# First projection weights loaded between the modulation's parts, modulation as columns, k tiles multiplied as they come

## The chip, the cores and the metric

The kernel runs on one core of a Trainium2 chip. Its engines work side by side, each through its own queue in order: TensorE (PE) multiplies, VectorE (DVE) and ScalarE (ACT) do the elementwise work, GpSimd (POOL) and SyncE (SP) mostly issue transfers. The metric is the device time of one execution in microseconds (us), as the median of several runs.

## The reference

One transformer layer for 512 tokens of width 1024 in f32: modulation from a condition vector, one projection to all branches, sparse attention and a state-space branch beside each other, their mix, and 32 experts of which each token takes four. The change touches its first lines only:

```python
cond = jax.nn.silu(c)
mod = cond @ w_ada[l] + b_ada[l]
sh_m, sc_m, g_m, sh_f, sc_f, g_f = jnp.split(mod[:, None, :], 6, axis=-1)
h = _rms(x, norm_mix[l]) * (1.0 + sc_m) + sh_m
proj = h @ w_in[l]
...
```

## The kernel before

A framework schedules the program: the source states the work, and the scheduler decides in which order each engine gets its instructions; the queues then run in that order and wait on semaphores. Tiles come from pools with few buffers (`raw`, `whi` and `wlo` have two each), and a tile's next use waits until the one before has been read.

*The modulation.* `sc_m` and `sh_m` are needed as columns (channel on the partition) in `mod1`: columns 8 to 15 hold the scale, 0 to 7 the shift. The weights come in four parts `early[j]`, j = 0 to 3, of 256 channels each; a part has a scale tile set `early[j][0]` and a shift tile set `early[j][1]` of 1 MB each. Their buffers are called bE (part 0, and again part 3), bV (part 1) and bD (part 2). `modulation(j)` computes the scale as a row, eight matmuls with `cond` as weights and 256 moving columns (L328), copies the row to SBUF on ACT (L330) and turns it into columns with matmuls against a one (L335). The shift is accumulated on DVE over the eight k tiles (`mac`, L255 and L257) and summed over partitions by L336. Three small DVE operations (L338 to L340) finish the part. An f32 matmul shows as two records in the trace.

*The input.* `xs0` (buffer bC) holds the 512 tokens as four tiles. ACT squares and sums them (L310), DVE computes the inverse root (L311, then `rsqrt`, L237 to L242) and scales bC (L314).

*The operand.* `modulate(j)` transposes channels 256 j to 256 j + 255 (L346; two k tiles, eight transposes), ACT applies scale and shift twice (L347 to the rounded high part in `hT[0]`, buffer bA; L349), and DVE subtracts for the low part (L350, buffer B).

*The projection.* A product of f32 quality is made of three matmuls of 512 columns (L356 to L358: high x high, low x high, high x low). `project` does so for a list of outputs and a list of k tiles. `first` is three outputs: 88 rows from `w_small` into bank sy, and two of 128 rows from `w_in[0]` into the banks mm: 8 x 3 x 3 = 72 matmuls. The last two outputs come from `w_in[1]` (banks ss): 48 matmuls. Weights are loaded by `load` (L176, on SP's queue, in the order of the source) and parted by `split` (L182 on ACT, L183 on DVE); `w_small` by `hilo` (L247, L248).

*Behind the stage.* The 88-row output is copied and transposed (L426, L433, L434), the index keys are normalized and transposed (L451), and the next weights are split by `advance`. From there on PE has projections, attention and experts up to the end.

Of the kernel before, what the change touches and what calls it, by code (L numbers as in the profile page):

```python
# [16 lines left out]
AF = mybir.ActivationFunctionType  # L17
OP = mybir.AluOpType
# [4 lines left out]
P = 128  # L23
# [3 lines left out]
KD = D // P  # L27
# [106 lines left out]
def program(tc, A, dbg=None, upto=99):  # L134
    nc = tc.nc
    V, S, T, G = nc.vector, nc.scalar, nc.tensor, nc.gpsimd
# [3 lines left out]
    with ctx:  # L140
# [14 lines left out]
        c_c, b_a1, nmix, gain, ssmn, convc, dskip = (cols[:, a:b] for a, b in (  # L155
            (0, 8), (8, 24), (24, 32), (32, 38), (38, 46), (46, 106), (106, 114)))
        identb = con.tile([P, P], BF, name="identb")
        V.tensor_copy(identb, ident)
        ones = con.tile([P, P], F32, name="ones")
# [14 lines left out]
        def load(src, n=2048, pool=None):  # L174
            raw = (pool or stm).tile([P, 2048], F32, name="raw", tag="raw", bufs=RAW)
            nc.sync.dma_start(raw[:, 0:n], src)  # L176
            return raw

        def split(raw, n=2048, pin=False):
            hi = stm.tile([P, 2048], F32R, name="whi", tag="whi", bufs=HI)  # L180
            lo = stm.tile([P, 2048], F32R, name="wlo", tag="wlo", bufs=LO)
            S.activation(hi[:, 0:n], raw[:, 0:n], AF.Copy)  # L182
            i = V.tensor_tensor(lo[:, 0:n], raw[:, 0:n], hi[:, 0:n].bitcast(F32), op=OP.subtract)  # L183
            if pin:
                tc.keep_in_program_order(i)
            return hi, lo
# [18 lines left out]
        with ExitStack() as c1:  # L205
# [4 lines left out]
            c0 = ExitStack()  # L210
            WE = c0.enter_context(tc.tile_pool(name="WE", bufs=1, side="right"))

            def big(tag, shape, dt=F32):
                return (WE if tag in ("E", "V", "V2", "SC", "S8") else W).tile(shape, dt, name=f"b{tag}", tag=tag, bufs=1)
# [7 lines left out]
            def r2(shape=(P, 512), dt=F32, name="r2"):  # L222
                return W.tile(list(shape), dt, name=name, tag="r2", bufs=R2)
# [4 lines left out]
            def sm(shape, dt=F32, name="sm", bufs=2):  # L228
                return W.tile(list(shape), dt, name=name, tag=name, bufs=bufs)

            def pt(tag, shape=(P, 512), dt=F32):
                return ps.tile(list(shape), dt, name=tag, tag=tag, bufs=PS[tag])
# [20 lines left out]
            def mac(acc, tiles):  # L253

                V.tensor_scalar(acc, part(tiles, 0), cond[:, 0:1], None, op0=OP.mult)  # L255
                for k in range(1, KD):
                    V.scalar_tensor_tensor(acc, part(tiles, k), cond[:, k:k + 1], acc, op0=OP.mult, op1=OP.add)  # L257
# [11 lines left out]
            def two(tag):  # L269
                t2 = big(tag, [P, 2, 2048])  # L270
                return [t2[:, 0]], [t2[:, 1]]

            early = [two("E"), ([big("V", [P, 2048])], [big("V2", [P, 2048])])]
# [5 lines left out]
            def ada_load(tiles, j):  # L279
                for i in range(2):  # L280
                    n = 2048 // len(tiles[i])
                    for h, tile_ in enumerate(tiles[i]):
                        nc.sync.dma_start(tile_, A["w_ada"][j + 4 * (1 - i)][:, h * n:(h + 1) * n])
                return tiles

            def part(tiles, k):
                n = KD // len(tiles)
                return tiles[k // n][:, (k % n) * 256:(k % n + 1) * 256]

            ada_load(early[0], 0)  # L290
            for t in range(NT):
                nc.sync.dma_start(xs0[:, t, :], xv[:, t, :])
            ada_load(early[1], 1)
            ada_load(early[2], 2)
            raws = [load(A["w_small"][0], KD * 88), load(A["w_in"][0])]
            heads = con.tile([P, 32], F32, name="heads")
            nc.scalar.dma_start(heads, _bcast(A["heads"], 32))
            rel = con.tile([32, 8], F32, name="rel")
# [3 lines left out]
            cond = con.tile([P, KD], F32, name="cond")  # L302
# [14 lines left out]
            wqi = [split(raws[1])]  # L317

            ada = pt("ac")
            mod1 = con.tile([P, 16], F32, name="mod1")  # L320
            psm = pt("sy")
            pqi = [pt("mm"), pt("mm"), pt("ss"), pt("ss")]

            def modulation(j):
                row = sm([1, 256], name="brow", bufs=1)
                p = ada[0:1, 256:512]
                for k in range(KD):
                    T.matmul(p, cond[:, k:k + 1], part(early[j][0], k),  # L328
                             start=(k == 0), stop=(k == KD - 1))
                S.activation(row, p, AF.Copy)  # L330
                acc = r2((P, 256))
                mac(acc, early[j][1])
                for b in range(2):
                    n = 2 * j + b
                    T.matmul(ada[:, 8 + n:9 + n], row[:, b * P:(b + 1) * P], ones[0:1, 0:1], start=True, stop=True)  # L335
                    T.matmul(ada[:, n:n + 1], acc[:, b * P:(b + 1) * P], ones[:, 0:1], start=True, stop=True)  # L336
                n = 2 * j
                V.tensor_tensor(mod1[:, 8 + n:10 + n], ada[:, 8 + n:10 + n], b_a1[:, 8 + n:10 + n], op=OP.add)  # L338
                V.tensor_tensor(mod1[:, n:n + 2], ada[:, n:n + 2], b_a1[:, n:n + 2], op=OP.add)
                V.scalar_tensor_tensor(mod1[:, 8 + n:10 + n], mod1[:, 8 + n:10 + n], 1.0, nmix[:, n:n + 2], op0=OP.add, op1=OP.mult)  # L340

            def modulate(j):
                for k in (2 * j, 2 * j + 1):
                    p = pt("at")
                    for t in range(NT):
                        T.transpose(p[:, t * P:(t + 1) * P], xs0[:, t, k * P:(k + 1) * P], ident)  # L346
                    S.activation(hT[0][:, k, :], p, AF.Identity, bias=mod1[:, k:k + 1], scale=mod1[:, 8 + k:9 + k])  # L347
                    f = r2()
                    S.activation(f, p, AF.Identity, bias=mod1[:, k:k + 1], scale=mod1[:, 8 + k:9 + k])  # L349
                    V.tensor_tensor(hT[1][:, k, :], f, hT[0][:, k, :].bitcast(F32), op=OP.subtract)  # L350

            def project(outs, ks):
                for k in ks:
                    for p, (wh, wl), step, c0, m in outs:
                        c = k * step + c0
                        T.matmul(p, wh[:, c:c + m], hT[0][:, k, :], start=(k == 0), stop=False)  # L356
                        T.matmul(p, wh[:, c:c + m], hT[1][:, k, :], start=False, stop=False)
                        T.matmul(p, wl[:, c:c + m], hT[0][:, k, :], start=False, stop=(k == KD - 1))  # L358

            first = [(psm[0:88, :], wsm, 88, 0, 88)] + [(pqi[c], wqi[0], 256, c * P, P) for c in range(2)]  # L360
            for j in range(4):
                modulation(j)
                if j == 0:
                    early.append(ada_load(two("E"), 3))
                    raws.append(load(A["w_in"][1]))
                if j > 0:
                    modulate(j - 1)
                if j > 1:
                    project(first, (2 * j - 4, 2 * j - 3))
            modulate(3)  # L370
            project(first, range(4, KD))
            wqi.append(split(raws[2]))
            for c in range(2, 4):
                project([(pqi[c], wqi[1], 256, (c % 2) * P, P)], range(KD))
            say("hT_hi", hT[0].bitcast(F32), [P, KD, L])
            for i in range(2):
                say(f"hT_lo{i}", hT[1].tiles[i].bitcast(F32), [P, 4, L])
# [53 lines left out]
            p = pt("at", (P, NT, P))  # L431
# [12 lines left out]
            for t in range(NT):  # L444
                for b in range(2):
                    V.tensor_scalar(kin[:, t, b * 64:(b + 1) * 64], s88[:, t, 0:64], mv[:, t, 0:1], rski[:, t:t + 1],
                                    op0=OP.subtract, op1=OP.mult)
            kiT = big("K", [P, L])
            p = pt("at")
# [563 lines left out]
            for half in range(2):  # L1013
# [3 lines left out]
                for j2 in range(2):  # L1017
# [4 lines left out]
                    for b in range(2):  # L1022
                        p = pt("mm")
# [13 lines left out]
            for j in range(4):  # L1037
# [9 lines left out]
                for b in range(2):  # L1047
# [3 lines left out]
                    p = pt("mm")  # L1051
# [126 lines left out]
            p = pt("mm")  # L1178
# [4 lines left out]
            p = pt("mm")  # L1183
# [392 lines left out]
        with ExitStack() as c3:  # L1576
# [10 lines left out]
            with tc.For_i(0, nb):  # L1587
# [72 lines left out]
                for n in range(2):  # L1660
                    p = op.tile([P, 512], F32, name="dn", tag="dn", bufs=2)
# [23 lines left out]
```

## Time and profile before

| what | value |
|---|---|
| median of three runs | 1811.93 us (1810.32 to 1813.92) |
| the profiled execution | 1815.36 us |
| its span | 1813.6 us, 22580 instructions |
| mean granted TensorE clock | 0.975 of full speed |

The profile is of one execution, which took 3.4 us more than the median. PE is busy for 97% of the span, DVE for 85% and ACT for 59%; the stage that the change touches is the first 70 us. In the views of the trace each line has a start and a length in us; an engine's idle time stands in brackets with what ended it, and a weight load (PEld) has its own lines beside the matmuls (PE).

### The profile page before, as it was taken

What the parts mean: (1) busy time and instruction counts of PE and PEld (TensorE: products, weight loads), DVE (VectorE), ACT (ScalarE), POOL (GpSimd) and SP (SyncE); (2) the same over time, 40 slices, a digit from 0 to 9 for tenths busy, and PEclk for the clock granted to TensorE, in tenths of its full rate; (3) what the DMA queues carried; (4) which work ended last, traced back from release to release, by engine and by line L of the source; (5) the groups of instructions that cost most, each with busy time, mean ns of one, the idle gap of its engine ahead of it and who ended that gap; (6) DMA issues with size and microseconds to landing.
All of it is one profiled execution on the core that took longest, in us unless ns stands there. A gap on an engine that the chain in (4) does not pass through costs nothing.

```text
span 1813.6 us, 22580 instructions
## 1 busy us (share of the span) xinstructions
PE 1752.4 (97%) x8534; PEld 1389.9 (77%) x8536; DVE 1542.5 (85%) x1886; ACT 1074.8 (59%) x1059; POOL 196.4 (11%) x115
## 2 busy tenths in 40 slices
PE   6999999999999798999999999999999999999997
PEld 3866877776678677888888888888888888888885
DVE  6477678875676789999999999999999999999996
ACT  3444333444323356777777777777777777777774
POOL 0000000000000101111211211111111111211112
PEclk9989999999799899999999999999999999999999
DMA  8232344432485489999999999999999999999993
GB/s 330 73 140 71 118 149 142 163 137 82 141 291 198 152 282 370 395 388 363 381 385 384 381 370 388 375 384 371 374 383 390 353 397 381 365 384 390 381 358 68
DMA packets 86600, 527.24 MB, mean 291 GB/s; under 512 B 10929, under 2 KB 11089, under 8 KB 32217
## 3 DMA queue, kind: packets, MB, share of 16 engines
q1 hardware_dynamic: 70552, 469.70, 66.3%
q0 software_dynamic: 15696, 55.97, 11.3%
q8 instruction: 68, 1.11, 0.2%
q14 instruction: 44, 0.35, 0.1%
q10 hardware_dynamic: 240, 0.10, 0.0%
HBM read 497.91 MB, written 30.45 MB: 291 GB/s over the span
## 4 chain that ended last, share of the span: by engine, by line
PE 88%; DVE 6%; DMA 3%; ACT 2%; issue 1%; SPq 0%; POOLq 0%; DVEq 0%; ACTq 0%
PE gu L1502 12%; PE gu L1500 12%; PE gu L1501 12%; PE dn L1500 7%; PE dn L1502 7%; PE dn L1501 6%; PE mm L393 4%; PE mm L394 4%; PE mm L395 4%; PE tr L1271 3%; PE gu L1511 2%; PE ac L850 1%; PE at L822 1%; DMA xg<-h2d,gi 1%; PE mm L385 1%
## 5 line engine op out<-in xcount | busy, mean ns | idle before, releaser
L1320 DVE TENSOR_TENSOR mlo<-raw,mhi 128x2048 fp32r<-128x2048 f32 (+1 forms) x160 | 352.2, 2205 | 24.3 <-ACT mhi L1319 22.4
L1320 DVE TENSOR_TENSOR wlo<-raw,whi 128x2048 fp32r<-128x2048 f32 x154 | 351.8, 2286 | 24.2 <-ACT whi L1319 22.5
L1319 ACT ACTIVATE whi<-raw 128x2048 fp32r<-128x2048 f32 x154 | 296.2, 1924 | 112.8 <-PE gu L1502 63.2
L1319 ACT ACTIVATE mhi<-raw 128x2048 fp32r<-128x2048 f32 (+1 forms) x160 | 296.6, 1859 | 104.8 <-PE gu L1502 58.4
L1501 PE MATMUL gu<-mlo,xh 128*128 128x512 f32 x496 | 193.3, 390 | 1.5 <-DVE mlo L1320 1.5
L1502 PE MATMUL gu<-whi,xl 128*128 128x512 f32 x496 | 193.8, 391 | 0.0
L1500 PE MATMUL gu<-mhi,xh 128*128 128x512 f32 x496 | 193.8, 391 | 0.0
L1502 PE MATMUL gu<-mhi,xl 128*128 128x512 f32 x496 | 193.8, 391 | 0.0
L1500 PE MATMUL gu<-whi,xh 128*128 128x512 f32 x496 | 193.8, 391 | 0.0
L1501 PE MATMUL gu<-wlo,xh 128*128 128x512 f32 x496 | 193.3, 390 | 0.0
L1290 POOL DMA_INDIRECT out_dram<-y,si x30 | 100.8, 3358 | 444.6 <-DVE y L1560 444.6
L394 PE MATMUL mm<-B,whi 128*128 128x512 f32 x352 | 141.9, 403 | 0.0
L393 PE MATMUL mm<-bA,whi 128*128 128x512 f32 x320 | 132.1, 413 | 2.0 <-DVE brow L662 1.0
L395 PE MATMUL mm<-bA,wlo 128*128 128x512 f32 x320 | 128.7, 403 | 0.8 <-DVE wlo L183 0.8
L182 ACT ACTIVATE whi<-raw 128x2048 fp32r<-128x2048 f32 x34 | 64.9, 1913 | 88.7 <-PE mm L394 74.8
L1377 POOL DMA_INDIRECT xg<-h2d,gi x32 | 59.7, 1866 | 503.0 <-PE tr L1271 479.5
L1501 PEld LDWEIGHTS gu<-mlo,xh 128*128 128x128 f32 x496 | 93.2, 188 | 22.2 <-DVE mlo L1320 1.9
L1501 PEld LDWEIGHTS gu<-wlo,xh 128*128 128x128 f32 x496 | 93.1, 188 | 20.4
L1502 PEld LDWEIGHTS gu<-mhi,xl 128*128 128x128 f32 x496 | 93.1, 188 | 20.2
L1502 PEld LDWEIGHTS gu<-whi,xl 128*128 128x128 f32 x496 | 93.1, 188 | 20.2
L1500 PEld LDWEIGHTS gu<-mhi,xh 128*128 128x128 f32 x496 | 93.1, 188 | 19.5
L1500 PEld LDWEIGHTS gu<-whi,xh 128*128 128x128 f32 x496 | 93.1, 188 | 19.3
(473 smaller groups left out, 3705.9 us busy)
## 6 DMA issues: line engine op xcount, KB each, us to landing
raw<-in_w_gu_dram SPq DMA_DIRECT2D x204, 1024.0 KB
raw<-in_w_dn_dram SPq DMA_DIRECT2D x104, 1024.0 KB
B<-in_w_gu_dram SPq DMA_DIRECT2D x52, 1024.0 KB
B<-in_w_dn_dram SPq DMA_DIRECT2D x24, 1024.0 KB
raw<-in_w_in_dram SPq DMA_DIRECT2D x23, 1024.0 KB
rawp<-in_w_ada_dram POOLq DMA_DIRECT2D x30, 512.0 KB, 4.1
bE<-in_w_ada_dram SPq DMA_DIRECT2D x4, 1024.0 KB
bC<-in_x_dram SPq DMA_DIRECT2D x8, 512.0 KB
```

The costliest lines, as they stand in the source:

```text
L182: S.activation(hi[:, 0:n], raw[:, 0:n], AF.Copy)
L393: T.matmul(p, wh, xT[0][:, k, :], start=(k == 0), stop=False)
L394: T.matmul(p, wh, xT[1][:, k, :], start=False, stop=False)
L395: T.matmul(p, wl, xT[0][:, k, :], start=False, stop=(k == nk - 1))
L1271: T.transpose(p[:, k, :], src[:, (4 * b + k) * P:(4 * b + k + 1) * P], ident)
L1290: return G.indirect_dma_start(out=out, out_offset=bass.IndirectOffsetOnAxis(ap=si, axis=0), in_=y, in_offset=None, compute_op=OP.add)
L1319: S.activation(hi[:, cs], raw[:, cs], AF.Copy)
L1320: i = V.tensor_tensor(lo[:, cs], raw[:, cs], hi[:, cs].bitcast(F32), op=OP.subtract)
L1377: G.indirect_dma_start(out=xg, out_offset=None, in_=h2d, in_offset=bass.IndirectOffsetOnAxis(ap=info[e][0], axis=0))
L1500: T.matmul(p, x[0][:, kk, :], hi[:, ws], start=(start and kk == 0), stop=False)
L1501: T.matmul(p, x[0][:, kk, :], lo[:, ws], start=False, stop=False)
L1502: T.matmul(p, x[1][:, kk, :], hi[:, ws], start=False, stop=(kk == KD - 1))
```

## The change

The scale of every part, and the shift of parts 0 and 1, are now computed as columns: for each half b and each k tile a 128x128 piece of the modulation's weights is the stationary operand and `cond[:, k]` the only moving column, 16 matmuls per tile set. The shifts of parts 2 and 3 stay on DVE. `w_small` and `w_in[0]` are loaded ahead of part 1's tile sets and `w_in[1]` ahead of part 2's. After each part, its two k tiles are transposed and multiplied into the first three outputs at once; at part 2 `w_in[1]` is split and its outputs start, with k tiles 0 to 3, then 4 and 5, and 6 and 7 at the end.

```diff
@@ -290,9 +290,10 @@
             ada_load(early[0], 0)
             for t in range(NT):
                 nc.sync.dma_start(xs0[:, t, :], xv[:, t, :])
+            raws = [load(A["w_small"][0], KD * 88), load(A["w_in"][0])]
             ada_load(early[1], 1)
+            raws.append(load(A["w_in"][1]))
             ada_load(early[2], 2)
-            raws = [load(A["w_small"][0], KD * 88), load(A["w_in"][0])]
             heads = con.tile([P, 32], F32, name="heads")
             nc.scalar.dma_start(heads, _bcast(A["heads"], 32))
             rel = con.tile([32, 8], F32, name="rel")
@@ -322,22 +323,25 @@
             pqi = [pt("mm"), pt("mm"), pt("ss"), pt("ss")]
 
             def modulation(j):
-                row = sm([1, 256], name="brow", bufs=1)
-                p = ada[0:1, 256:512]
-                for k in range(KD):
-                    T.matmul(p, cond[:, k:k + 1], part(early[j][0], k),
-                             start=(k == 0), stop=(k == KD - 1))
-                S.activation(row, p, AF.Copy)
-                acc = r2((P, 256))
-                mac(acc, early[j][1])
-                for b in range(2):
-                    n = 2 * j + b
-                    T.matmul(ada[:, 8 + n:9 + n], row[:, b * P:(b + 1) * P], ones[0:1, 0:1], start=True, stop=True)
-                    T.matmul(ada[:, n:n + 1], acc[:, b * P:(b + 1) * P], ones[:, 0:1], start=True, stop=True)
                 n = 2 * j
+
+                def columns(c0, tiles):
+                    for b in range(2):
+                        for k in range(KD):
+                            T.matmul(ada[:, c0 + b:c0 + b + 1], part(tiles, k)[:, b * P:(b + 1) * P], cond[:, k:k + 1],
+                                     start=(k == 0), stop=(k == KD - 1))
+
+                columns(8 + n, early[j][0])
                 V.tensor_tensor(mod1[:, 8 + n:10 + n], ada[:, 8 + n:10 + n], b_a1[:, 8 + n:10 + n], op=OP.add)
+                V.scalar_tensor_tensor(mod1[:, 8 + n:10 + n], mod1[:, 8 + n:10 + n], 1.0, nmix[:, n:n + 2], op0=OP.add, op1=OP.mult)
+                if j < 2:
+                    columns(n, early[j][1])
+                else:
+                    acc = r2((P, 256))
+                    mac(acc, early[j][1])
+                    for b in range(2):
+                        T.matmul(ada[:, n + b:n + b + 1], acc[:, b * P:(b + 1) * P], ones[:, 0:1], start=True, stop=True)
                 V.tensor_tensor(mod1[:, n:n + 2], ada[:, n:n + 2], b_a1[:, n:n + 2], op=OP.add)
-                V.scalar_tensor_tensor(mod1[:, 8 + n:10 + n], mod1[:, 8 + n:10 + n], 1.0, nmix[:, n:n + 2], op0=OP.add, op1=OP.mult)
 
             def modulate(j):
                 for k in (2 * j, 2 * j + 1):
@@ -358,20 +362,21 @@
                         T.matmul(p, wl[:, c:c + m], hT[0][:, k, :], start=False, stop=(k == KD - 1))
 
             first = [(psm[0:88, :], wsm, 88, 0, 88)] + [(pqi[c], wqi[0], 256, c * P, P) for c in range(2)]
+            second = []
             for j in range(4):
                 modulation(j)
+                ks = 2 * j, 2 * j + 1
                 if j == 0:
                     early.append(ada_load(two("E"), 3))
-                    raws.append(load(A["w_in"][1]))
-                if j > 0:
-                    modulate(j - 1)
-                if j > 1:
-                    project(first, (2 * j - 4, 2 * j - 3))
-            modulate(3)
-            project(first, range(4, KD))
-            wqi.append(split(raws[2]))
-            for c in range(2, 4):
-                project([(pqi[c], wqi[1], 256, (c % 2) * P, P)], range(KD))
+                if j == 2:
+                    wqi.append(split(raws[2]))
+                    second += [(pqi[c], wqi[1], 256, (c % 2) * P, P) for c in range(2, 4)]
+                    project(second, range(4))
+                if j == 3:
+                    project(second, (4, 5))
+                modulate(j)
+                project(first, ks)
+            project(second, (6, 7))
             say("hT_hi", hT[0].bitcast(F32), [P, KD, L])
             for i in range(2):
                 say(f"hT_lo{i}", hT[1].tiles[i].bitcast(F32), [P, 4, L])
```

Three places show how the engines' orders move. The lines of the kernel after have moved by one to five: its columns are L331, its transposes L350, its projection L360 to L362.

DVE, before, from the end of part 0's shift to the start of the inverse root (`mod_170` is `mod1`, `r_186` the accumulator):

```order
L307 TENSOR_TENSOR cond<-cols,ce 128x8
L255 TENSOR_SCALAR r_186<-bE,cond 128x256
L257 SCALAR_TENSOR_TENSOR r_186<-bE,cond,r_186 128x256 x7
L338 TENSOR_TENSOR mod_170<-ac,cols 128x2
L339 TENSOR_TENSOR mod_170<-ac,cols 128x2
L340 SCALAR_TENSOR_TENSOR mod_170<-mod_170,cols 128x2
L311 TENSOR_SCALAR ss<-ss 128x4
L237 TENSOR_SCALAR rxy<-ss 128x4
```

DVE after, at the same place (`mod_172` is `mod1`; L344 adds the shift; L248 is the split of `w_small`):

```order
L307 RECIPROCAL ce<-ce 128x8
L308 TENSOR_TENSOR cond<-cols,ce 128x8
L335 TENSOR_TENSOR mod_172<-ac,cols 128x2
L336 SCALAR_TENSOR_TENSOR mod_172<-mod_172,cols 128x2
L344 TENSOR_TENSOR mod_172<-ac,cols 128x2
L312 TENSOR_SCALAR ss<-ss 128x4
L237 TENSOR_SCALAR rxy<-ss 128x4
L238 TENSOR_SCALAR rxy<-rxy 128x4
L240 TENSOR_TENSOR rxt<-rxy 128x4
L241 SCALAR_TENSOR_TENSOR rxt<-rxt,ss 128x4
L248 TENSOR_TENSOR r_164<-raw,r_163 128x704
L242 SCALAR_TENSOR_TENSOR rxy<-rxt,rxy 128x4
```

The accumulation is gone, the shift's add L344 stands ahead of `ss`, and the split of `w_small` stands inside the inverse root.

PE, before, from its first instruction (`at` is a bank for transposes, bC the input, bV and bE modulation weights):

```order
L328 MATMUL ac<-bE,cond 1x256 x8
L335 MATMUL ac<-ones,brow 128x1
L336 MATMUL ac<-ones,r_186 128x1
L335 MATMUL ac<-ones,brow 128x1
L336 MATMUL ac<-ones,r_186 128x1
L328 MATMUL ac<-bV,cond 1x256 x8
L346 MATMUL at<-cst,bC 128x128 x4
L335 MATMUL ac<-ones,brow 128x1
L346 MATMUL at<-cst,bC 128x128 x4
```

PE after, from its first instruction (`x15` counts matmuls):

```order
L331 MATMUL ac<-cond,bE 128x1 x32
L350 MATMUL at<-cst,bC 128x128 x8
L331 MATMUL ac<-cond,bV 128x1 x15
L360 MATMUL sy<-bA,r_163 88x512
L360 MATMUL mm<-bA,whi 128x512 x2
L331 MATMUL ac<-cond,bV 128x1
L350 MATMUL at<-cst,bC 128x128 x4
L361 MATMUL sy<-B_104,r_163 88x512
L362 MATMUL sy<-bA,r_164 88x512
L361 MATMUL mm<-B_104,whi 128x512
```

All 32 column matmuls of part 0 come first, then eight transposes, which need bC, and only then part 1's columns and the first projection matmuls; before, part 1's row stood ahead of the transposes.

DVE, before, at the end of the stage (`sy` is the 88-row output, `bS_498` its transposed copy; L183 splits the next weights):

```order
L350 TENSOR_TENSOR B_105<-r_381,bA 128x512
L350 TENSOR_TENSOR B_105<-r_390,bA 128x512
L426 COPY r_491<-sy 88x512
L183 TENSOR_TENSOR wlo<-raw,whi 128x2048
L434 COPY bS_498<-at 128x352
L439 BN_STATS kst<-bS_498 128x6 x2
```

DVE after, at the same place (`bS_524` is the transposed copy):

```order
L354 TENSOR_TENSOR B_105<-r_465,bA 128x512
L354 TENSOR_TENSOR B_105<-r_474,bA 128x512
L431 COPY r_517<-sy 88x512
L183 TENSOR_TENSOR wlo<-raw,whi 128x2048
L439 COPY bS_524<-at 128x352
L444 BN_STATS kst<-bS_524 128x6 x2
```

The last two low parts of the operand now stand right ahead of the copy of the 88 rows, and one split of the next weights stands between that copy and the transposed copy, as before, but with no projection behind it.

## Rows read from the trace of the kernel before

**Rows 1.** The page: its span line and part 1, busy time by engine.
```profile
span 1813.6 us, 22580 instructions
PE 1752.4 (97%) x8534; PEld 1389.9 (77%) x8536; DVE 1542.5 (85%) x1886; ACT 1074.8 (59%) x1059; POOL 196.4 (11%) x115
```

**Rows 2.** Stretches: from:to, length, busy (x count) per engine, PEclk, DMA share, GB/s.
```profile
9.30:24.70 15.40, 12.13 (x40) 4.50 (x40) 9.84 (x30) 4.64 (x9) 0.00 (x0) 0.89 1.02 414
20.10:23.50 3.40, 3.40 (x9) 1.00 (x8) 3.26 (x8) 0.00 (x0) 0.00 (x0) 0.51 0.99 399
33.80:69.70 35.90, 35.90 (x171) 26.54 (x171) 16.38 (x26) 15.28 (x20) 0.00 (x0) 1.00 0.37 135
102.00:115.70 13.70, 13.67 (x43) 9.14 (x44) 8.53 (x12) 4.48 (x9) 0.10 (x1) 0.50 0.41 143
115.70:1813.00 1697.30, 1653.08 (x8064) 1321.40 (x8065) 1472.59 (x1678) 1029.31 (x983) 195.35 (x110) 0.98 0.80 298
451.20:454.60 3.40, 3.40 (x17) 3.38 (x17) 0.64 (x4) 1.43 (x4) 0.00 (x0) 0.50 0.01 1
454.60:477.50 22.90, 22.57 (x70) 13.86 (x71) 11.67 (x37) 5.42 (x11) 1.05 (x2) 0.50 0.16 52
```

**Rows 3.** Timeline of PE (matmuls): start, length, line, out<-in, shapes, count.
```profile
28.95 3.61 PE L328 MATMUL ac<-bD,cond 128*1 128x256 f32 x16 [0.39 <-DVE mod L339]
33.80 0.48 PE L356 MATMUL sy<-bA,r 128*88 128x512 f32 x1
58.43 0.39 PE L356 MATMUL ss<-bA,whi 128*128 128x512 f32 x1
69.29 0.40 PE L358 MATMUL ss<-bA,wlo 128*128 128x512 f32 x1
```

**Rows 4.** Timeline of PE's weight loads, within the first L328 group.
```profile
12.75 0.13 PEld L328 LDWEIGHTS ac<-bE,cond 128*1 128x1 f32 x1 [0.30 <-issue]
13.17 0.13 PEld L328 LDWEIGHTS ac<-bE,cond 128*1 128x1 f32 x1 [0.30 <-issue]
13.46 0.95 PEld L328 LDWEIGHTS ac<-bE,cond 128*1 128x1 f32 x5 [0.16 <-issue]
```

**Rows 5.** Timeline of PE at two later places with one-column matmuls.
```profile
451.40 2.99 PE L891 MATMUL sy<-ones,bSC 128*128 128x1 f32 x14
584.91 0.67 PE L1180 MATMUL mm<-bfc,bK 128*32 128x1 f32 x16
```

**Rows 6.** Chain of waits: start, length, what.
```profile
48.70 0.31 PE ac L335 x2
49.33 0.93 PE at L346 x8
69.69 0.32 PE at L433 x4
76.77 0.30 PE at L451
```

**Rows 7.** Timeline of DVE in the first 70 us.
```profile
12.25 3.61 DVE L257 SCALAR_TENSOR_TENSOR r<-bE,cond,r 128x256 f32<-128x256 f32 x7
18.48 0.17 DVE L311 TENSOR_SCALAR ss<-ss 128x4 f32<-128x4 f32 x1 [1.10 <-ACT r L310]
20.86 2.74 DVE L314 TENSOR_SCALAR bC<-bC,rxy 128x1024 f32<-128x1024 f32 x4
32.89 0.88 DVE L248 TENSOR_TENSOR r<-raw,r 128x704 fp32r<-128x704 f32 x1
60.40 2.29 DVE L183 TENSOR_TENSOR wlo<-raw,whi 128x2048 fp32r<-128x2048 f32 x1 [2.46 <-ACT whi L182]
```

**Rows 8.** Timeline of ACT; in brackets the idle time before and its releaser.
```profile
50.07 0.78 ACT L347 ACTIVATE bA<-at,mod 128x512 fp32r<-128x512 f32 x1 [2.68 <-DVE mod L340]
```

**Rows 9.** Timeline of SP's queue: start, length, loads issued.
```profile
33.80 6.66 SPq L176 DMA_DIRECT2D raw<-in_w_in_dram  x2
```

**Rows 10.** Timeline of PE behind 100 us, with the idle time before.
```profile
101.17 0.43 PE L522 MATMUL ac<-da,cst 128*128 128x64 f32 x2 [1.49 <-DVE da L517]
```


## The prediction

> **What bounds the kernel now.** I read the page first. PE is busy for 1752.4 of 1813.6 us [rows 1], so a delay of PE's work is a delay of the end unless PE has idle time behind it. The profiled execution took 1815.4 us, 1.8 us more than its span and 3.4 us more than the median of 1811.9; I sum against 1815.4 and take 3.4 off at the end. About 0.2% (3.6 us) is what a measurement of this kernel can tell from no change.
>
> Then I cut the start into stretches [rows 2]. Until 24.7 us the transfers are the limit: their engines are full (share 1.02, 414 GB/s) while PE is busy for 12.1 of 15.4 us. From 33.8 us, where the first projection matmul starts [rows 3], to 69.7 us PE has no gap at all (35.90 of 35.90). After 115.7 PE is busy for 1653 of 1697 us. So this stage's end is set by two things: when the projection can start, and how much PE work is left from there. What is late at 70 us is late at the end: nothing behind the stage is tied to a fixed time.
>
> **Prices.** TensorE has two levels here, 1.2 and 2.4 GHz. The first row-form scale (L328) shows both: its weight loads follow each other every 0.42 us from 9.4 on, and from 13.4 five of them take 0.95, 0.19 each [rows 4]. So it works for 4 us at the lower level before the rise. The third L328 group, at the full level, took 3.61 us for 16 records, 0.226 each [rows 3].
>
> The new form is the opposite shape: 128x128 weights and one moving column. No row of this stage has such records in number, but 14 stand back to back at L891: 2.99 us, 0.213 each, at a granted 0.50, the lower level [rows 5]. A tile set of 16 matmuls is 32 records: **6.8 us at the lower level, half of it, 3.4 us, at the full one**. The half agrees with the transposes, whose weights are as large: 8 in 0.93 us, 0.116 each [rows 6]. Bounds at the full level: above, L335's 0.31 us for two records (0.155 each, +1.5 us per tile set) [rows 6]; below, L1180's one-column records with 32 columns of weights, 16 in 0.67 us, 0.042 each [rows 5]. I take 0.107, from the row of the same shape.
>
> **The change, part by part.** *Removed:* four L328 groups (3.6 us each at the full level), their ACT copies, the L335 matmuls, and for parts 0 and 1 the DVE accumulation, whose last seven steps alone are 3.61 us [rows 7]. DVE is no limit here, so what it saves only counts where PE waits for it. *Added:* six tile sets as columns, at the full level 20.5 us, against 4 x 3.61 = 14.4.
>
> *(a) Part 0.* Its matmuls start at 9.4 us as before. Before, the first 4 us ran at the lower level and a rise followed work of 256 moving columns. In the L891 stretch the granted clock stayed at 0.50 through the column records and for the 22.9 us behind, though PE was busy for 22.57 of them [rows 2, 5]. So being busy did not lift it there, and I take it that columns don't lift it here: scale 9.4 to 16.2, shift to 23.0.
>
> *(b) What is queued behind it.* On DVE the shift's add (L344) now stands ahead of the RMS chain (ss, rsqrt, then the four scalings of bC), which does not need it. Before, that chain ran from 18.48 to 23.60, 5.1 us [rows 7]; now it begins behind L344 at 23.2 and has the split of w_small (L248, 0.88) inside it, and the last bC is there at 29.2. On PE eight transposes that need bC stand ahead of part 1's columns, so PE idles from 23.0 and they are done at 29.4. Only then come 30 of the 32 records of part 1's scale, 6.4 us at the lower level. **The first projection matmul starts at 35.8 instead of 33.8.**
>
> *(c) Work left from there, at the full level.* 120 projection matmuls at 0.231 (the last 48 of before start between 58.43 and 69.29 [rows 3]) = 27.7; 24 transposes 2.8; three column sets and a matmul 10.5; two accumulator tails with four one-column matmuls at 0.31, 1.2. That is 42.2 us. The same stretch before was 35.9. Two waits that I find in the new order and that nothing covers: part 1's first matmul needs ACT's 0.78 us after the shift's columns, and part 3's needs L343, DVE and then ACT, as before at 50.07 [rows 8], about 0.9. Sum 1.7. End at 35.8 + 42.2 + 1.7 = 79.7.
>
> *(d) The clock.* The first projection matmuls still run at the lower level until it rises: about as long as at 9.4 us, 4 us, which costs half, 1.8. Each of the three later column sets is 3.4 us of one-column records. If each drops the clock for as long as the shortest lower stretch I find, 20.1 to 23.5 [rows 2], it costs 1.7 each, 5.1; if none does, 0. I take two of three, 3.4. **Stage end 84.9 instead of 69.7, +15.2.**
>
> *(e) The tail.* Before, the next weights' split (DVE L183, 2.29 us) ran at 60.4, hidden under `second`, since `first` had ended; now both end together, its buffers come free only at the end, and in DVE's order it stands ahead of the copy on the way to the keys' transposes (69.69 to 76.77 before [rows 6, 7]). Between nothing and the whole 2.29 shows; I take 1.5, since ACT's part of the split must come first. **+16.7.**
>
> *(f) Loads.* At 414 GB/s a 1-MB tile takes 2.5 us. In the new order w_small, w_in[0] and part 1 (3.4 MB) lie behind x, whose last tile is summed by 18.48, so they are there by 27, before PE wants part 1 at 29.4. w_in[1] waits on SP for the reading of w_small by L248, at about 26, and holds parts 2 and 3 behind it, as two loads took 6.66 us on it before [rows 9]. Parts 2 and 3 are there by about 40, PE wants part 2 at about 47: hidden. If PE came 7 us earlier, 2 to 3 us of it would show.
>
> The profiled execution would take 1815.4 + 16.7 = 1832.1, the median 1828.7. With the clock kept through all later sets it is 5 us less; with 0.155 per record about 5 us more.
>
> **Rivals.**
> *R1, the columns lift the clock like any work.* Then part 0's scale ends at about 14.8, its shift at 18.2 and the RMS chain is as early as before: bC done at 24.5 with L248, part 1's scale at 27.9 to 29.6, since PE idles 6 us before it, which lowered the clock before as well (0.51 in 20.1 to 23.5). With 42.2 + 1.7 the stage ends at 71.8 to 73.5, and with the tail the shift is +3.6 to +5.3. For it: L328 lifted the clock, and PE is as busy with columns. Against it: the L891 stretch [rows 5]. The Trainium skill's page "TensorE: Matmul & The Clock Gate", Part 1, says that throttling is the default and recent busyness releases it, not a count of instructions; by that rule R1 is what happens. Median 1815.5 to 1817.2, 1819 with 2 us of waiting for loads (f). Chance 0.20.
>
> *R2, not slower.* R1, and the lower stretch from 102 to 115.7 us (13.7 us at 0.50 [rows 2]) goes away. It follows PE's idle 1.49 us in front of L522, where it waits for DVE [rows 10]; if the shifted streams close that gap, up to half of 13.7, 6.8 us, comes back: 5.3 - 6.8 = -1.5, 1810.4. It decides once more than 1.8 us of it comes back in R1. Against it: what releases that wait is a DVE chain that is delayed along with PE. Chance 0.07.
>
> *R3, a one-column record costs only its issue,* near L1180's 0.042: a tile set is 1.3 us, part 0 is done by 14, bC at 24.5, the first projection matmul at 26.1; behind it 27.7 + 2.8 + 4.2 + 1.2 + 1.7 = 37.6, stage end 63.7; with 1.5 of tail and 1 of lower clock -3.5: 1808.4. "TensorEngine Tiling (Array Packing)" in the Trainium skill, on instruction overhead, has a very short free size cost no less than that overhead, and no more; its figure would lead here. L891's 0.213 with the same weights contradicts it. Chance 0.03.
>
> That the change has no effect is no case: the orders differ, and the PE work is larger.
>
> **How the numbers follow.** Forecast 0.70 (own range 1822 to 1836), R1 0.20, R2 0.07, R3 0.03. The prediction is the forecast's 1828.7. The range leaves out R2, R3 and a little of the forecast's top: 1815.5 to 1835. Slower by over 0.2% holds the forecast and nearly all of R1's 0.20 (0.88), within 0.2% most of R2 and R1's lowest edge (0.07), faster 0.05.
>
> **What would show it.** Right: L331's 32 records of part 0's scale take 6 to 7 us, its shift ends near 23; DVE's ss waits for L344; transposes near 29; first projection matmul near 36; 512-column matmuls at 0.43 behind column sets; the 88-row transposes near 85. Wrong: the sets take 3.4 us from the second on (R1) or 1.2 (R3); PE waits for a load of parts 1 to 3; or the lower stretch behind 102 us is gone.

## The result

The kernel after took 1835.17 us (median of four, 1833.14 to 1837.59), the kernel before on the same occasion 1812.35: a ratio of 1.013, interval 1.0104 to 1.0157. It is slower, as forecast, but by 22.8 us, where 16.7 were forecast; the range ended 0.2 us short of it. Timed again on another occasion, the same program had a median of 1829.98 against 1813.01, 1.0104 (1.0078 to 1.0129), 17.0 us more and inside the range. The profiled execution has a span of 1833.5 us, 19.9 more than that of before [rows 1].

The page of the kernel after, span and part 1:

```profile
span 1833.5 us, 22763 instructions
PE 1771.2 (97%) x8638; PEld 1417.1 (77%) x8640; DVE 1534.8 (84%) x1870; ACT 1073.7 (59%) x1055; POOL 196.5 (11%) x115
```

PE has 18.8 us more busy time than before, of which the six sets at the full level would explain 6 (20.5 against 14.4). The timeline of PE shows where the rest is (`L331` are the columns, `bC` the scaled input, `sy` the 88-row output):

```profile
9.70 6.96 PE L331 MATMUL ac<-cond,bE 128*128 128x1 f32 x32 [9.70 <-DMA bE<-in_w_ada_dram]
16.91 6.99 PE L331 MATMUL ac<-cond,bE 128*128 128x1 f32 x32 [0.25 <-DVE mod L335]
27.89 2.67 PE L350 MATMUL at<-cst,bC 128*128 128x128 f32 x8 [3.99 <-DVE bC L315]
30.35 6.40 PE L331 MATMUL ac<-cond,bV 128*128 128x1 f32 x30
36.61 0.71 PE L360 MATMUL sy<-bA,r 128*88 128x512 f32 x1
39.57 0.62 PE L362 MATMUL sy<-bA,r 128*88 128x512 f32 x1
40.00 0.43 PE L361 MATMUL mm<-B,whi 128*128 128x512 f32 x1
43.03 3.63 PE L331 MATMUL ac<-cond,bV 128*128 128x1 f32 x32
47.72 0.73 PE L360 MATMUL sy<-bA,r 128*88 128x512 f32 x1 [0.42 <-ACT bA L351]
91.11 0.47 PE L438 MATMUL at<-cst,r 88*128 88x88 f32 x4
124.00 0.43 PE L527 MATMUL ac<-da,cst 128*128 128x64 f32 x2 [1.50 <-DVE da L522]
```

Part 0's two column sets take 6.96 and 6.99 us; then PE idles for 3.99 us and the transposes wait for bC tile by tile. The first projection matmul (sy) starts at 36.61 (33.80 before [rows 3]). There, 512-column matmuls that follow each other start 0.43 us apart up to 40.00, and 0.23 apart from 40.26 on. One set, at 43.03, has the full level and takes 3.63 us. The 88-row transposes, which end the stage, start at 91.11 (69.69 before [rows 6]: the chain counts a record from when the one before ends), and the decay matmul (L527, L522 before) at 124.00, 22.8 us later than before, behind the same wait of 1.5 us [rows 10].

DVE at the start and at the end of the stage:

```profile
23.93 0.16 DVE L344 TENSOR_TENSOR mod<-ac,cols 128x2 f32<-128x2 f32 x1 [6.88 <-PE ac L331]
24.01 0.16 DVE L312 TENSOR_SCALAR ss<-ss 128x4 f32<-128x4 f32 x1
24.90 0.89 DVE L248 TENSOR_TENSOR r<-raw,r 128x704 fp32r<-128x704 f32 x1
27.08 2.74 DVE L315 TENSOR_SCALAR bC<-bC,rxy 128x1024 f32<-128x1024 f32 x4
90.72 2.29 DVE L183 TENSOR_TENSOR wlo<-raw,whi 128x2048 fp32r<-128x2048 f32 x1 [2.44 <-ACT whi L182]
92.93 0.52 DVE L439 COPY bS<-at 128x352 f32<-128x352 f32 x1
```

The RMS chain starts at 24.01, behind L344, which waits for the second set; before, it started at 18.48 [rows 7]. L248 lies inside it. At the end the split of 2.29 us stands ahead of the copy on the way to the keys.

The stretches of PE (from:to, length, busy and count by engine, PEclk, DMA share, GB/s; PEclk is the mean granted clock, 1.00 at 2.4 GHz, and a stretch at 0.50 is called lower):

```profile
9.70:23.90 14.20, 13.95 (x64) 13.77 (x64) 0.32 (x2) 7.19 (x10) 0.00 (x0) 1.00 1.01 412
46.50:57.10 10.60, 10.18 (x34) 7.92 (x34) 3.83 (x4) 4.59 (x5) 0.00 (x0) 0.52 0.21 70
57.10:60.20 3.10, 3.10 (x28) 2.98 (x26) 0.00 (x0) 0.00 (x0) 0.00 (x0) 1.00 0.71 278
60.20:63.90 3.70, 3.70 (x13) 2.97 (x13) 3.36 (x9) 0.00 (x0) 0.00 (x0) 0.54 0.00 0
68.20:72.70 4.50, 4.50 (x35) 4.50 (x33) 0.00 (x0) 2.34 (x4) 0.00 (x0) 0.79 0.00 0
72.70:77.60 4.90, 4.90 (x14) 3.76 (x15) 4.53 (x11) 0.00 (x0) 0.00 (x0) 0.50 0.00 0
77.60:91.10 13.50, 13.05 (x61) 9.97 (x60) 3.18 (x7) 5.60 (x8) 0.00 (x0) 1.00 0.00 1
121.50:140.00 18.50, 16.80 (x65) 10.81 (x65) 13.16 (x27) 8.78 (x17) 0.80 (x1) 0.72 0.50 179
```

In the first stretch PE is busy for 13.95 of 14.20 us and still takes 0.218 us per record. The view's 1.00 there is no measurement: it shows 1.00 also from 36.6 to 40.0, where the matmuls above start 0.43 us apart against 0.23 later, so at the start the record spacing tells the level. From 46.5 on there are three lower stretches at three column sets, 10.2, 3.4 and 6.8 us long (10.6 us at 0.52 is 10.2 at 0.50 and the rest at 1.00, and so on); two begin right behind a set, the third at 70.8, within the last one. The projection matmuls lie in them.

The only load that PE waited for in this stage, and the one load on SP that is held:

```profile
PE ac L331 <- DMA bE<-in_w_ada_dram: 9.7, 1, 9.7
```

```profile
25.82 0.33 SPq L176 DMA_DIRECT2D raw<-in_w_in_dram  x1
```

`w_in[1]` was issued at 25.82, when L248 had read `w_small`, and held six loads; PE never waited for one of them.

### The profile page after: what moved, and what is told of

Read it like the earlier page. It is cut to its first block, busy times and chain, and to the rows that moved or that the text cites. A ratio compares the mean times of both kernels' runs of the same rounds, so it can differ in the third digit from the quotient of the medians.

```text
span 1833.5 us, 22763 instructions
## 1 busy us (share of the span) xinstructions
PE 1771.2 (97%) x8638; PEld 1417.1 (77%) x8640; DVE 1534.8 (84%) x1870; ACT 1073.7 (59%) x1055; POOL 196.5 (11%) x115
## 4 chain that ended last, share of the span: by engine, by line
PE 89%; DVE 6%; DMA 3%; issue 1%; ACT 1%; SPq 0%; POOLq 0%; DVEq 0%; ACTq 0%
PE gu L1507 12%; PE gu L1505 12%; PE gu L1506 12%; PE dn L1505 6%; PE dn L1507 6%; PE dn L1506 6%; PE mm L398 4%; PE mm L399 4%; PE mm L400 4%; PE tr L1276 3%; PE ac L331 2%; PE gu L1516 2%; PE ac L855 1%; PE at L827 1%; DVE wlo L183 1%
## 5 line engine op out<-in xcount | busy, mean ns | idle before, releaser
L1505 PEld LDWEIGHTS gu<-mhi,xh 128*128 128x128 f32 x496 | 93.1, 188 | 19.5
```

Of the source, the lines that this page charges most:

```text
L1505: T.matmul(p, x[0][:, kk, :], hi[:, ws], start=(start and kk == 0), stop=False)
```

## The experiments

Two theories stood against each other. **A**: column sets (the 16 matmuls of a tile set as columns) keep TensorE at its lower level and drop it again behind each set. **B**: the order costs the time (moved loads, part-by-part k tiles, waits), whatever form the modulation has.

**e1_rows** undoes the columns only: `modulation` is that of the kernel before, in the kernel after.

```diff
-                columns(8 + n, early[j][0])
...
+                for k in range(KD):
+                    T.matmul(p, cond[:, k:k + 1], part(early[j][0], k),
+                             start=(k == 0), stop=(k == KD - 1))
```

> The kernel after with the modulation of the kernel before (scale as a row of 256 moving columns, shift accumulated on DVE); loads and the order of the k tiles stay as in the kernel after. Theory A (the column sets hold TensorE at its lower level and drop it again behind each set): no column sets, so the inverse root starts near 18.5 again, the first projection matmul near 26 to 28, 45 us of PE work behind it at the full level, the 88-row transposes at 71 to 75 instead of 91; median 1813 to 1819. Rival B (the moved loads and the k tiles multiplied part by part make PE wait, whatever form the modulation has): transposes at 85 or later, median 1828 or more.

Measured: 1.002 (0.9988 to 1.0052), no difference from before. Its first projection matmul and its 88-row transposes, on PE's timeline:

```profile
26.11 0.73 PE L357 MATMUL sy<-bA,r 128*88 128x512 f32 x1
73.97 0.47 PE L435 MATMUL at<-cst,r 88*128 88x88 f32 x4
```

Both are where A has them (26 to 28, 71 to 75). B falls: loads and k-tile order alone cost the stage some 4 us, and of the end no more than the interval allows, 0.5%.

**e2_cols** is the other half: columns in the kernel before, with its loads and order.

```diff
-                    T.matmul(p, cond[:, k:k + 1], part(early[j][0], k),
...
+                columns(8 + n, early[j][0])
```

> The kernel before with the modulation of the kernel after (columns for all scales and the shifts of parts 0 and 1); loads and the order of the k tiles stay as in the kernel before. Theory A: parts 0 and 1 run at the lower level, 6.8 us per tile set, the projection starts after 40, the 88-row transposes come 10 to 18 us later than before; median 1822 to 1832. Rival B: the order of before hides the columns under loads, median 1811 to 1816.

Measured: 1.0105 (1.0072 to 1.0137), 1829.8. Two of its first four sets, and the transposes:

```profile
23.24 6.99 PE L330 MATMUL ac<-cond,bV 128*128 128x1 f32 x32 [0.25 <-DVE mod L343]
31.83 6.83 PE L330 MATMUL ac<-cond,bV 128*128 128x1 f32 x32
89.51 0.47 PE L436 MATMUL at<-cst,r 88*128 88x88 f32 x4
```

All four sets of parts 0 and 1 take 6.8 to 7.0 us, one behind the other. The transposes come 20 us later than before, two more than the upper end of the expectation. The columns by themselves make nearly the whole loss.

**e3_loads** moves the loads alone.

```diff
+            raws = [load(A["w_small"][0], KD * 88), load(A["w_in"][0])]
             ada_load(early[1], 1)
+            raws.append(load(A["w_in"][1]))
             ada_load(early[2], 2)
```

> The kernel before with the moved loads alone (w_small, w_in[0] ahead of part 1, w_in[1] ahead of part 2). Theory A: no column sets, so the stage ends within 3 us of before; median 1809 to 1816. Rival B: SP waits for the split of w_small ahead of part 2's loads and PE waits for them, median 1817 or more.

Measured: 1.0005 (0.998 to 1.003): no difference.

**e4_wide** keeps the source order and the number of matmuls and weight loads, but multiplies 128 equal columns and reads the result from one of them:

```diff
-                            T.matmul(ada[:, c0 + b:c0 + b + 1], part(tiles, k)[:, b * P:(b + 1) * P], cond[:, k:k + 1],
+                            T.matmul(ada[:, 256 + b * P:256 + (b + 1) * P], part(tiles, k)[:, b * P:(b + 1) * P],
+                                     cond[:, k:k + 1].to_broadcast([P, P]), start=(k == 0), stop=(k == KD - 1))
...
```

> The kernel after with cond[:, k] repeated over 128 moving columns in the column matmuls (as many matmuls and weight loads as in the kernel after, each with 128 moving columns in place of one; the result is taken from one of the columns). Theory A, in the form that what counts for the level is moving columns: the level rises within 4 us of the first set, sets take 3.4 to 4 us, and no lower stretch follows a set, so the 88-row transposes come at 72 to 78 instead of 91; median 1815 to 1821. Rival (weight loads of 128x128 for short matmuls cost 6.8 us or the sets drop the level whatever moves): median 1832 or more.

Measured: 1.0041 (1.0025 to 1.0057), 1820.9. PE's timeline:

```profile
8.65 6.41 PE L331 MATMUL ac<-cond,bE 128*128 128x128 f32 x32 [8.65 <-DMA bE<-in_w_ada_dram]
15.31 3.84 PE L331 MATMUL ac<-cond,bE 128*128 128x128 f32 x32 [0.25 <-DVE mod L336]
36.65 3.84 PE L331 MATMUL ac<-cond,bV 128*128 128x128 f32 x32
75.74 0.47 PE L440 MATMUL at<-cst,r 88*128 88x88 f32 x4
```

and its stretches:

```profile
36.60:40.50 3.90, 3.90 (x36) 3.86 (x35) 2.37 (x2) 0.00 (x0) 0.00 (x0) 1.00 0.65 237
40.50:57.00 16.50, 16.50 (x98) 13.97 (x97) 5.54 (x15) 4.30 (x7) 0.00 (x0) 1.00 0.23 91
57.00:75.70 18.70, 18.26 (x99) 14.68 (x98) 7.73 (x17) 6.84 (x10) 0.00 (x0) 1.00 0.00 1
```

The second set takes 3.84 us in place of 6.99, and a set later on, 36.65 to 40.5, has no lower stretch behind it: 1.00 to the end of the stage, which comes 15.4 us earlier than in the kernel after. With 128 times the moving work the sets are faster. This is the run that shows the cause, most directly for part 0: its 64 records stand first in both kernels, with the same weight loads and the same wait between the sets, and what differs is the moving columns (and with them the columns written). From part 1 on the scheduled order differs as well, since most column matmuls stand between projection matmuls here; the set at 36.65 is the one that still stands in one piece. One lower stretch is left that the trace records, from 24.4 to 31.2; it lies behind the 3.99 us in which PE waits for bC, not behind a set.

**after2** is the kernel after, unchanged; its profile was taken to see what repeats.

> The kernel after once more, unchanged, for a second profile of it. The stage should repeat within 0.5 us (first projection matmul 36.6, 88-row transposes 91.1, the decay matmul L527 at 124.0). Theory C (behind the stage the lower stretches fall otherwise from execution to execution, or with when PE gets there): the index-count matmuls L1185, at 604.6 in the first profile, differ by 1.5 us or more here. Rival D (behind the stage the order alone decides): they repeat within 1 us.

Its stretches, and PE's timeline at three places:

```profile
47.60:56.50 8.90, 8.33 (x31) 6.56 (x31) 3.83 (x4) 4.59 (x5) 0.00 (x0) 0.62 0.10 16
66.50:73.20 6.70, 6.70 (x42) 6.11 (x41) 2.61 (x7) 2.32 (x4) 0.00 (x0) 0.75 0.00 0
121.50:140.00 18.50, 18.11 (x97) 12.41 (x98) 15.40 (x29) 10.92 (x26) 0.11 (x1) 1.00 0.50 183
```

```profile
41.94 0.62 PE L361 MATMUL sy<-B,r 128*88 128x512 f32 x1
42.37 0.43 PE L362 MATMUL sy<-bA,r 128*88 128x512 f32 x1
87.79 0.47 PE L438 MATMUL at<-cst,r 88*128 88x88 f32 x4
120.68 0.43 PE L527 MATMUL ac<-da,cst 128*128 128x64 f32 x2 [1.51 <-DVE da L522]
```

The projection started at 36.4, but the transposes at 87.79 in place of 91.11, and the index-count matmuls L1185 (L1180 before) at 596.7 in place of 604.6: C for this program, within the stage too, against my expectation that it repeats. The level rises 2.4 us later than in the first profile (matmuls 0.43 apart up to 42.37). The lower stretches at the sets are shorter here (6.8 us at 47.6 to 56.5, 3.4 at 66.5 to 73.2) and only two in number, and the one behind the decay matmul, in which the first profile has 0.72, is not there at all, though PE waited 1.51 us ahead of it as always.

**e5_shift0** puts part 0's shift back on DVE, and nothing else.

```diff
-                if j < 2:
+                if j == 1:
```

> The kernel after with the shift of part 0 alone accumulated on DVE, as before, in place of its second column set. In the order of DVE the accumulation stands behind the scale's two operations, which wait for the first column set (16.7 in the kernel after), so it runs from 16.9 to 21, and the inverse root starts near 21.5 instead of 24.0. Theory A with step (b) (the inverse root is late because it is queued behind the shift's add): everything up to the end of the stage moves by these 2.5 us, first projection matmul near 34, 88-row transposes near 88.5; median 1830 to 1834. Rival (the chain behind the start does not set the end of the stage): transposes stay at 91 or within 1 us of it.

DVE's start of the RMS chain, then PE's first projection matmul, the 88-row transposes and the decay matmul:

```profile
21.20 0.16 DVE L312 TENSOR_SCALAR ss<-ss 128x4 f32<-128x4 f32 x1
```

```profile
33.81 0.71 PE L360 MATMUL sy<-bA,r 128*88 128x512 f32 x1
86.33 0.47 PE L438 MATMUL at<-cst,r 88*128 88x88 f32 x4
119.21 0.43 PE L527 MATMUL ac<-da,cst 128*128 128x64 f32 x2 [1.49 <-DVE da L522]
```

The chain starts 2.8 us earlier than in the kernel after and the projection starts 2.8 us earlier, as step (b) has it. The stage ends 4.8 us earlier, more than the lead, since the lower stretches fall otherwise; yet the profiled execution ends later (span 1837.0 against 1833.5), and the median shows no gain (1835.6, ratio 1.012, 1.0095 to 1.0145). It was run again for that:

> The kernel of e5_shift0 once more, for a second profile. Its stage ended 4.8 us earlier than that of the kernel after, but its end was 3.5 us later. Theory C: the lead of about 4.8 us at the decay matmul L527 (119.2) repeats, and what is left of it at L1185 and at the end differs from the first profile by more than 1.5 us. Rival D (something in its order behind the stage costs it the lead): the loss between L527 and L1185 repeats within 1 us (487.6 us from one to the other).

```profile
88.79 0.47 PE L438 MATMUL at<-cst,r 88*128 88x88 f32 x4
```

The second time the projection started at 33.82, and the lead of 2.8 us there repeats. The ends of the stage by themselves would not show it: 86.33 and 88.79 here, 91.11 and 87.79 in the two profiles of the kernel after. The second profile is like the first of the kernel after in its time at the lower level (granted clock 0.80 over 38.0 to 88.8, and over 40.0 to 91.1 there), and against that one it is 2.3 us ahead. From the decay matmul to L1185 it took 487.8 us, as the first time (487.6): D, not C, by the two profiles. But its four executions took 1827.4, 1827.5, 1834.3 and 1841.5 us, and the profile is of the longest. So the two profiles are of long executions, and what decides behind the stage stays open. The medians, 1835.6 and 1830.9, cannot be told from those of the kernel after, 1835.2 and 1830.0.

**e6_late** has columns for the scales of parts 2 and 3 alone.

```diff
+            def modulation(j):
+                (rows if j < 2 else cols_)(j)
```

> The kernel after with parts 0 and 1 in the old form and columns for the scales of parts 2 and 3 alone (two sets of six). Against e1_rows (88-row transposes at 74.0) it tells how much of the loss is the level behind the later sets and how much the start. Theory A: a lower stretch follows each of the two sets, of 3 to 7 us, which costs 1.7 to 3.5 each, less 1.6 for the shorter PE work: 76 to 79; median 1818 to 1823. Rival (all of the loss is at the start, the level recovers at once): 72 to 74, median as e1_rows or lower.

Measured: 1.0041 (1.0024 to 1.0057), 1820.5. The stretches around its two sets (37.6 to 41.6 and 54.0 to 57.6), and the transposes:

```profile
40.00:48.00 8.00, 8.00 (x28) 6.27 (x28) 5.10 (x12) 0.00 (x0) 0.00 (x0) 0.57 0.31 126
48.00:54.00 6.00, 6.00 (x33) 5.03 (x32) 0.16 (x1) 0.23 (x1) 0.00 (x0) 1.00 0.00 0
54.00:62.00 8.00, 8.00 (x48) 6.95 (x47) 4.13 (x10) 2.55 (x4) 0.00 (x0) 0.79 0.01 2
```

```profile
75.22 0.47 PE L459 MATMUL at<-cst,r 88*128 88x88 f32 x4
```

A lower stretch of 6.9 us begins within the first set, at 40.8, and one of 3.4 us right behind the second; the 48 to 54 between is full. The transposes came at 75.2, a little under the expectation, 1.2 later than in e1_rows although PE has less to do.

**e7_mac3** and **e8_mac23** come from the other way to take rows off PE: accumulate the scale on DVE like the shift, for part 3, and for parts 2 and 3, in the kernel before.

```diff
+                if j > 1:
+                    row = r2((P, 256))
+                    mac(row, early[j][0])
+                else:
```

> The kernel before with the scale of part 3 accumulated on DVE as its shift is, in place of the row of eight matmuls (3.6 us of PE). PE has no gap from 33.8 to 69.7 and DVE is busy for 16.4 of these 35.9 us, so PE's work should go down by 3.6 us with the DVE work hidden: 88-row transposes at 66 to 67 instead of 69.5, median 2 to 4 us lower, 1808 to 1810.5 on the scale of 1812.4. Rival: part 3's scale is late on DVE and PE waits for it: no change, or up to 2 us slower.

> As e7_mac3, for the scales of parts 2 and 3 (7.2 us of PE). If DVE keeps up: 88-row transposes at 63 to 65, median 5 to 7 us lower, 1805 to 1807. Rival: from 29 to 40 DVE has 8 us of accumulation and 6 of other work, part 2's scale and the low parts of the operand come late, and PE waits for a part of the 7.2 us or for more: 66 to 70, median 1809 to 1813.

Measured: 0.9975 (0.9961 to 0.9988) for part 3, transposes at 66.84; 0.9965 (0.9951 to 0.9978) for both, 66.28. The first is as expected. The second falls to its rival by the transposes (66 to 70), though its median, 1807.1, is near what was forecast: of its 7.2 us PE gives back more than half; two of its waits and the transposes:

```profile
33.57 0.73 PE L362 MATMUL sy<-bA,r 128*88 128x512 f32 x1 [0.22 <-DVE r L248]
39.15 0.73 PE L362 MATMUL mm<-bA,wlo 128*128 128x512 f32 x2 [0.75 <-DVE wlo L183]
66.28 0.47 PE L437 MATMUL at<-cst,r 88*128 88x88 f32 x4
```

From 24 to 40 us PE is busy for 12.26 of 16.00 us: among other things it waits for the splits on DVE (L248, L183), which stand between the accumulations there.

**e9_loads_mac** and **e10_come_mac** add the change's loads, or its loads and its order of k tiles, to e8_mac23.

```diff
+            raws = [load(A["w_small"][0], KD * 88), load(A["w_in"][0])]
             ada_load(early[1], 1)
...
+                if j == 2:
+                    wqi.append(split(raws[2]))
...
+                modulate(j)
+                project(first, ks)
```

> e8_mac23 (kernel before, scales of parts 2 and 3 accumulated on DVE) with the moved loads of the change. In e8_mac23 PE has waits between 25 and 37 us, the last of them for the parting of w_small and of w_in[0], which come late there; with the loads moved they are there by 27. If these waits go: 88-row transposes at 62 to 64 instead of 66.3, median 2 to 4 us under that of e8_mac23, a ratio of 0.994 to 0.996 to the kernel before. Rival: the accumulations on DVE are what PE waits for, and DVE has the same work: transposes at 66 or later, ratio as e8_mac23 or above.

> e1_rows (the change without its columns: moved loads, k tiles as they come) with the scales of parts 2 and 3 accumulated on DVE. e1_rows had the 88-row transposes at 74.0; less 7.2 us of PE work they come at 67 to 68, ratio 0.996 to 1.000. Rival: PE waits for the accumulations, since each part's k tiles are wanted as soon as the part is there: 70 to 74, ratio 1.000 to 1.004.

Measured: 0.9973 (0.9961 to 0.9986), transposes at 65.5, half a us short of the rival's 66 and with its ratio, so nearer to the rival; 0.997 (0.9954 to 0.9986), transposes at 66.1, 1 us earlier than expected, the ratio as expected. Neither can be told from e8_mac23. All four are 0.25 to 0.35% below the kernel before, and so below the kernel after too; what helps in them is the DVE sum.

## Why the prediction missed

Step (d) failed, in its size; the path and the other steps held up to the end of the stage.

*(a) Part 0 at the lower level:* right. 6.96 and 6.99 us against 6.8, and e4_wide shows that it is the one moving column. The price at the full level, 3.63, is near the 3.4 taken from the lower row.

*(b) The queue behind it:* right. Chain at 24.01 (forecast 23.2), last bC done at 29.8 (29.2), first projection matmul at 36.61 (35.8); 0.3 of the 0.8 is that the first load came later. e5_shift0 moved it as the step says, in both of its profiles.

*(c) PE work and waits:* near. The two waits for ACT came, 0.4 us each, 0.85 in place of 1.7. What is left of the 54.5 us from 36.61 to 91.11, without the waits and the clock's 11.9 of (d), is 41.8 of work against 42.2; the two accumulator tails took 0.36 us each, not 0.62.

*(d) The clock:* **this step failed, in its size.** I counted 1.8 us for the level's first rise and 3.4 for drops behind two of three sets, each for as long as the shortest lower stretch of the kernel before. The first part held here: matmuls 0.43 apart up to 40.0, 1.7 us. But all three sets had a lower stretch, and the three sum to 10.2 + 3.4 + 6.8 = 20.4 us, which cost half, 10.2. That is 6.8 us more than forecast, and the miss at the decay matmul is 6.1 (16.7 forecast, 22.8 measured); the 0.8 of (b) and the 0.85 of (c) cancel by luck, and the smaller work of (c) is most of the rest. Taking the shortest stretch as the length was the mistake; the kernel before itself has one of 13.7 us [rows 2]. The upper bound had the same length for all three sets and was too low for the same reason. How long a stretch gets differs from execution to execution. In after2 two of three sets had one, as counted, but for 6.8 and 3.4 us, which cost 5.1; the first rise came at 42.4 and cost 3.0. So the clock took 11.9 us in the first profile and 8.1 in the second, against 5.2 forecast, and the stage of after2 was 3.3 us shorter. The line that the clock kept through all later sets saves 5 us does not follow from this step either: by its own sum that is 3.4, or 5.2 with the first rise.

*(e) The tail:* right. The keys' first transpose came at 99.61, 22.84 us later than before [rows 6], while the 88-row transposes came 21.4 to 21.6 later: 1.3 to 1.4 against 1.5. The split ran from 90.72 to 93.0, ahead of the copy, as the step says.

*(f) Loads:* right, hidden, with the hold on SP at 25.82 as forecast. *From the stage to the end:* 22.8 at the decay matmul, 19.9 at the end of the first profile; 19.5 and 11.6 in after2. So "what is late at 70 us is late at the end" did not hold: 2.9 and 7.9 us came back, where the mean granted clock from the decay matmul to L1185 was 0.95 and 0.96, against 0.94 before.

*The median* is 6.5 us above the forecast. Of these, 3.2 are the profiled execution, 1835.3 against 1832.1: the 6.1 of the stage, less the 2.9 that came back behind it, which I had not foreseen. The other 3.3 are the 3.4 that I took off at the end, because the profiled execution of before lay 3.4 above its median; that of the kernel after lay at its median. On the second occasion the median was 1.3 us above the forecast. So whether the time came out inside the range hung on the occasion, and the sizes of step (d) were too low on both.

*R1* (columns lift the clock): refuted by the 13.95 busy of 14.20 us at 0.218 per record. The Trainium skill's rule, in "TensorE: Matmul & The Clock Gate", Part 1, that recent busyness releases the throttle, doesn't hold here for busy in the profile's sense. *R2's* effect did occur in after2, where the stretch behind the decay matmul stayed at 1.00, but not for the reason given, since the idle 1.5 us was there. *R3:* refuted, 0.109 per record at the full level.

## What to carry to other kernels

Before a product is turned so that the large operand becomes the weights and one column moves, look for a row of that shape and for the level it runs at: a busy PE with one moving column ran at the lower level, and left the long matmuls behind it there. If a price hangs on a lower stretch, take its length from all such stretches of the trace, the long ones too. A matrix times one vector went better to an engine with idle time in that stretch: part 3's scale on DVE took 0.25% off the kernel before. Adding part 2's made no difference that can be told from that.

## What the runs showed that I had not expected

More moving columns made the same matmuls faster: 3.84 us per set with 128 columns, 6.99 with one, by the level alone (one column at the full level takes 3.63). Nothing was run between one and 128. And one program differs from execution to execution by where its lower stretches fall: behind the same idle 1.5 us, the kernel after had 0.72 in one profile and 1.00 in the other over 121.5 to 140 us, and its eight executions lie between 1827.1 and 1837.6 us. What decides that was not found.
